# A hybrid attention and mLSTM network on one core: T4's low part by an adding DMA, keys' copies on GpSimd, and another order of the mLSTM heads' steps

## The chip, the cores and the metric

One core of a Trainium2 chip runs the whole program. TensorE (PE) multiplies; VectorE (DVE), ScalarE (ACT) and GpSimd (POOL) work on tiles; SyncE (SP) issues transfers, and so does GpSimd. Each engine works through its own instructions in their order and waits on the others by semaphores. The metric is the device time of one execution in microseconds (us). Of the kernel before, three runs are known.

## What is computed

```
h = x
h = h + dilated_attention_mixer(rms_norm(h, attn_norm[0]), positions, attn_w_in[0], attn_w_out[0])
h = h + swiglu(rms_norm(h, ffn_norm[0]), ffn_w_in[0], ffn_w_out[0])
h = h + mlstm_mixer(rms_norm(h, mlstm_norm[0]), mlstm_w_in[0], mlstm_conv_w[0], mlstm_conv_b[0],
                    mlstm_ig_bias[0], mlstm_fg_bias[0], mlstm_head_gain[0], mlstm_w_out[0])
h = h + swiglu(rms_norm(h, ffn_norm[1]), ffn_w_in[1], ffn_w_out[1])
return rms_norm(h, final_norm)

def swiglu(xn, w_in, w_out):
    gu = xn @ w_in
    return (jax.nn.silu(gu[..., :D_FF]) * gu[..., D_FF:]) @ w_out
```

512 tokens, a width of 1024. The attention has 8 heads of 128 in three groups of dilation 1, 4 and 16, with rotary turns of the first 32 of each head's dimensions. The mLSTM mixer has 8 heads too: queries and keys (64 wide) come out of a causal convolution with silu, each head's weights are exp of a difference of gate sums, times the scores, and its output is the weighted values over a denominator, normalized per head.

## The kernel before

Each fp32 operand is kept as a high and a low part, both of a rounded fp32 type; a product takes three matmuls (high by high, high by low, low by high). The high part is a copy that rounds (ACT); the low part is the difference to the raw value, as a rule one DVE operation.

**Feed-forward input.** From the column blocks j4 on, weights and tokens are multiplied with seven half-size products in place of eight (P1 to P7, `products`): sums and differences of weight blocks (A11 ... S4) times those of token blocks (B11 ... T4). The weight operands are made for each pair of blocks by `prepare` (load on SP, sum on DVE, high part on ACT, low part on DVE), the token operands once in each layer by `normalized`, whose steps are called between the products. `split_tokens` makes an operand's two parts. For B11 and T1 it uses the second way that it has (L1518 to L1520): ACT writes minus the high part, and an accumulating DMA issued by GpSimd adds the raw value. T4 is the last token operand and is read by the last product, P4. Its raw value T4 lies in the tile f0x (f1x in the second layer), whose buffer the weights of a later pair take (tag w8). In the trace the products of weights j4 are f0j_c, f0j_p and f0j_u; P2 adds into f0j_c, P7 and P4 into f0j_u, and between products ACT copies f0j_u out (f0j4u, L1680).

**Attention.** For each pair of heads the queries and keys of each group are projected, turned in `rope` and copied back into the operand tiles by the function `back` that `rope` returns. Group 0's copies go to GpSimd (L638), those of groups 1 and 2 to ACT (L642): 32 partitions by 512 elements for each of two queries' and two keys' halves (a1g_q, a1g_k in pair 1). Quarters 0 and 1 are the queries, 2 and 3 the keys. The copies are followed by the scores a1s (L781).

**mLSTM.** For each head hh `decay` makes the exponentials of gate differences (a matmul mHHnb into one bank, a mask on DVE, mHHd, ten exponentials on ACT, mHHe), `scores` makes queries times keys (mHHs, eight matmuls into two banks in turn) and multiplies them into mHHe on DVE (L2229), and `numerators` makes the weighted values (mHHnum, two banks of two), then a denominator, ACT's squares mHHj, a short row of DVE operations and the scaled output mHHyt (L2261). These steps are put off by `at_tick` to ticks that advance with the projections. Entries due at one tick run in the order in which they were queued. HEAD_AT gives the three ticks of each head:

```
HEAD_AT = ((9, 10, 12), (10, 11, 13), (12, 13, 15), (13, 14, 16), (15, 16, 18), (16, 17, 19), (18, 19, 21),
           (19, 20, 21))
```

A scheduler then sets the final order on each engine from the order in which the program issues and from its own estimate of times.

Of the kernel before, what the change touches and what calls it, by code (L numbers as in the profile page):

```python
# [40 lines left out]
HEAD_AT = ((9, 10, 12), (10, 11, 13), (12, 13, 15), (13, 14, 16), (15, 16, 18), (16, 17, 19), (18, 19, 21),  # L41
           (19, 20, 21))
# [32 lines left out]
def tile_hybrid_dilated_attn_mlstm(  # L75
# [4 lines left out]
    nc = tc.nc  # L80
# [336 lines left out]
    with ExitStack() as actx:  # L417
# [5 lines left out]
        R = 32  # L423
# [180 lines left out]
        def halves(t, th):  # L604
            return t[:, :, th * HALF:(th + 1) * HALF]
# [11 lines left out]
        def rope(qk, rot, blocks, first=0, end=4, direct=False):  # L617

            at = slice(R * first, R * end)
            a, sh = rot[0][at], rot[1][at]  # L620
            nc.vector.stream_shuffle(sh, a, shift)
            nc.vector.tensor_tensor(a, a, cosn[at], op=ALU.mult)
            nc.vector.tensor_tensor(sh, sh, sinn[at], op=ALU.mult)
            two_m = lambda t: t.rearrange("p (m s) -> p m s", m=2)
            if direct:
                for q in range(first, end):
                    nc.vector.tensor_tensor(halves(qk[q // 2][:R], q % 2), two_m(rot[0][quarter(q)]),
                                            two_m(rot[1][quarter(q)]), op=ALU.add)
                return
            nc.vector.tensor_tensor(a, a, sh, op=ALU.add)  # L630

            def back(by_pool=False):
                for q in range(first, end):
                    if blocks:
                        for m in range(2):
                            to, src = turned(qk, q, m, True), packed(rot, q, m, True)
                            if by_pool:
                                nc.gpsimd.tensor_copy(to, src)  # L638
                            else:
                                nc.scalar.activation(to, src, AF.Copy)  # L640
                    else:
                        nc.scalar.activation(halves(qk[q // 2][:R], q % 2), two_m(rot[0][quarter(q)]), AF.Copy)  # L642
            return back
# [325 lines left out]
        def qk_unit(pr, g, qk, then=None):  # L969
# [5 lines left out]
            rot = vu = None  # L975
# [51 lines left out]
            for n, name in enumerate(QK_ORDER):  # L1027
                key = target[name]
                if name in ("P1", "P5"):
                    acc[key] = acc_tile(nm + key)  # L1030
                if name == "P5":
                    acc["u"] = acc_tile(nm + "u")
                    nc.scalar.activation(acc["u"], acc["c11"], AF.Copy)
                    if g:
                        ahead_of_casts[0] = last_on(ACT)
                    feed.fill(feed.ahead + 1)
                whl = feed.pop()
                with fenced():
                    for m in range(2):
                        for k in range(4):  # L1040
                            for a, b in SPLITS:
                                if name in ("P1", "P2", "P4"):
                                    x_ = pair[b][k + 4 * (name != "P1")][:, HALF * (name == "P4"):HALF * (1 + (name == "P4"))]
                                else:
                                    x_ = sum_part(name, b, k)
                                nc.tensor.matmul(acc[key][:, m * HALF:(m + 1) * HALF], whl[a][:, k, m * P:(m + 1) * P], x_,
                                                 start=(name in ("P1", "P5") and m == 0 and k == 0 and (a, b) == SPLITS[0]),
                                                 stop=(m == 1 and k == 3 and (a, b) == SPLITS[-1]), skip_group_check=True)
                finish(name)
                if pr == 0:  # L1050
                    if g == 1:
                        if n == 0:
                            renew(range(4, 8))
                        elif n < 3:
                            sum_of("S%d" % (n + 2))
                        elif n == 6:
                            back = rope(qk, rot, False)
                            defer(1, lambda: behind(back, engine=ACT))
                            for key, hf in (("W11", 1), ("W12", 0), ("W12", 1), ("W22", 0), ("W22", 1)):
                                behind(load_block, 0, key, hf, engine=mybir.EngineType.SP)  # L1060
                    elif n == 6:
                        postponed.append(lambda: rope(qk, rot, False)())
                    if n in (1, 5):
                        advance()
                    continue
                if g == 2 and n == 2:
                    feed.ahead = 2
                if n == 6:
                    with behind_scores() if g == 2 else nullcontext():
                        back = rope(qk, rot, g == 0)  # L1070
                    if g == 0:
                        defer(1, lambda: back(True))
                    elif g == 2:
                        ahead_of_splits[0] = last_on(DVE)
                        back()
                        ahead_of_casts[0] = last_on(ACT)
                    else:
                        defer(1, lambda: behind(back, engine=ACT))
                if g == 2 and n == 5:
                    late[0] = last or by_products(pr + 1, 0)  # L1080
                    feed.fill(feed.ahead + 1)
                    late[0] = False
                if n in (1, 3, 5, 6):
                    advance()
                if n == 6 and then is not None:
                    then()
                if n:
                    feed.fill(feed.ahead + 1)
# [396 lines left out]
    def ffn_in(layer, fp, pair, rbc, hook, following, hid, during):  # L1485
# [27 lines left out]
        def split_tokens(key, by_dma=False):  # L1513

            i = [b for _, b in PRODUCTS].index(key)
            hi, lo = ops[key] = [op_tile(2 * i + part, key + "hl"[part]) for part in range(2)]
            nc.scalar.activation(hi, raw[key], AF.Copy)
            if by_dma:  # L1518
                nc.scalar.activation(lo, hi.bitcast(F32), AF.Copy, scale=-1.0)
                nc.gpsimd.dma_start(lo, raw[key], accum_op=ALU.add)  # L1520
            else:
                nc.vector.tensor_tensor(lo, raw[key], hi.bitcast(F32), op=ALU.subtract)

        def normalized():
            xs = [fp.tile([P, 4, SEQ], F32, tag="w8", name="f%dx%d" % (layer, i), bufs=2) for i in range(2)]
            for i in range(2):
                for t in range(2):
                    raw["B%d%d" % (i + 1, t + 1)] = xs[i][:, :, t * HALF:(t + 1) * HALF]
            for k in range(KC):
                nc.vector.scalar_tensor_tensor(xs[k // 4][:, k % 4], h[k], col("ffn", layer * KC + k), rbc,  # L1530
                                               op0=ALU.mult, op1=ALU.mult)
                yield
            split_tokens("B11", True)
            raw["T1"] = fp.tile([P, 4, HALF], F32, tag="t1", name="f%dt1" % layer)
            nc.vector.tensor_tensor(raw["T1"], raw["B12"], raw["B11"], op=ALU.subtract)
            yield

            split_tokens("T1", True)
            raw["T3"] = raw["B12"]
            nc.vector.tensor_tensor(raw["T3"], raw["B22"], raw["B12"], op=ALU.subtract)  # L1540
            yield
            split_tokens("T3")
            yield
            split_tokens("B22")
            yield
            raw["T2"] = raw["B22"]
            nc.vector.tensor_tensor(raw["T2"], raw["B22"], raw["T1"], op=ALU.subtract)
            split_tokens("T2")
            yield

            split_tokens("B21")
            yield

            raw["T4"] = raw["B21"]
            nc.vector.tensor_tensor(raw["T4"], raw["B21"], raw["T2"], op=ALU.subtract)
            split_tokens("T4")

        steps = normalized()
        STEPS = 2
# [461 lines left out]
    with ExitStack() as mctx:  # L2021
# [261 lines left out]
        def at_tick(t, fn):  # L2283
            defer(base + t - tick[0], fn)
        at_tick(8, exponents)
        for p, t in enumerate(STACK_AT):
            at_tick(t, lambda p=p: stack(p))
        for n, fn in enumerate((decay, scores, numerators)):
            for hh, ts in enumerate(HEAD_AT):
                at_tick(ts[n], lambda hh=hh, fn=fn: fn(hh))  # L2290
        for hh, t in LAST_OUTPUTS.items():
            at_tick(t, lambda hh=hh: outputs(hh))
        for pr, cs in ((2, (0, 2)), (3, (1, 3))):
# [254 lines left out]
```

## Time and profile before

| | us |
|---|---|
| median of 3 runs | 1383.32 (1382.18 to 1385.1) |
| the profiled execution | 1381.85 |
| its span | 1380.1 |
| attention with its output projection (awo) | 0 to 480 |
| first feed-forward (f0j on) | 480 to 846 |
| mLSTM mixer (mqk on) | 846 to 1038 |
| second feed-forward (f1j on) and the final norm | 1038 to 1380 |

The view of waits for TensorE lists each tile for which it stood still and what ended that wait; timelines show single instructions with their start; the view of windows shows each engine's busy time in a stretch. Line numbers are those of the kernel before; behind L634 the change adds two.

### The profile page before, as it was taken

The page shows a single profiled execution, that of the slowest core. Times are in us where ns is not written, and L with a number is a line of the kernel's source. Part 1 is how long each engine was busy: PE and PEld are TensorE (multiplying, and loading weights), DVE is VectorE, ACT ScalarE, POOL GpSimd, SP SyncE. Part 2 cuts the span into 40 slices and gives each one's busy share as a digit, 9 for nine tenths or more (in the row PEclk, how much of TensorE's full clock was granted, in tenths as well). Part 3 has the DMA queues.
Part 4 walks back from the last instruction along what each step waited for, and adds up shares of the span by engine and source line. Part 5 has one row for each costly group of instructions (what it writes and reads, how often), then busy time and mean ns, then how long its engine had stood idle before and what let it go on. Part 6 is the DMA issues. An engine that isn't in the chain of part 4 may idle for free. (4 is left out here: it accounts for less than half of the span.)

```text
span 1380.1 us, 23153 instructions
## 1 busy us (share of the span) xinstructions
PE 1363.8 (99%) x9028; PEld 1253.3 (91%) x9028; DVE 1127.4 (82%) x1782; ACT 806.2 (58%) x1297; POOL 183.0 (13%) x264
## 2 busy tenths in 40 slices
PE   9999999999999999999999999999999999999998
PEld 7898889999998889999999998888888899999886
DVE  7988668897975598788778799899858988887887
ACT  6766566777673444444476364786534544458854
POOL 3000013030402010000010110123102230001213
PEclk9999999999999999999999999999999999999999
DMA  9354245365576356323361743324334553335963
GB/s 311 112 176 137 92 139 184 130 183 169 172 264 208 105 139 167 123 73 111 123 167 63 168 125 92 92 64 121 92 123 122 148 174 115 123 113 131 200 162 106
DMA packets 140214, 193.85 MB, mean 140 GB/s; under 512 B 8996, under 2 KB 105060, under 8 KB 140104
## 3 DMA queue, kind: packets, MB, share of 16 engines
q1 hardware_dynamic: 120128, 140.73, 32.3%
q0 software_dynamic: 18752, 51.43, 15.4%
q8 instruction: 71, 1.16, 0.4%
q10 hardware_dynamic: 1224, 0.21, 0.1%
q14 instruction: 39, 0.32, 0.1%
HBM read 167.30 MB, written 22.54 MB: 138 GB/s over the span
## 5 line engine op out<-in xcount | busy, mean ns | idle before, releaser
L1805 POOL DMA_DIRECT2D f1T<-in_ffn_w_out_dram x15 | 17.8, 1185 | 207.7 <-DMA f1P_2w_w<-in_ffn_w_out_dram 136.4
L1780 POOL DMA_DIRECT2D f0S<-in_ffn_w_out_dram x10 | 8.7, 874 | 259.3 <-DVE f0hid L1697 173.2
L2337 POOL DMA_DIRECT2D hD<-hB x32 | 21.7, 697 | 68.5 <-DVE hB L2334 68.5
L268 PE MATMUL mo<-n_h,mo_k_l 128*128 128x512 f32 x64 | 25.3, 395 | 0.0
L268 PE MATMUL mo<-n_l,mo_k_h 128*128 128x512 f32 x64 | 25.2, 393 | 0.0
L268 PE MATMUL awo<-ao_h,awo_k_h 128*128 128x512 f32 x64 | 25.2, 393 | 0.0
L268 PE MATMUL mqk<-n_h,mqk_k_h 128*128 128x512 f32 x64 | 25.2, 393 | 0.0
L268 PE MATMUL mwo<-yo_l,mwo_k_h 128*128 128x512 f32 x64 | 25.1, 393 | 0.0
L268 PE MATMUL mo<-n_h,mo_k_h 128*128 128x512 f32 x64 | 25.1, 392 | 0.0
L268 PE MATMUL awo<-ao_h,awo_k_l 128*128 128x512 f32 x64 | 25.1, 391 | 0.0
L268 PE MATMUL f1j<-n_h,f1j_h 128*128 128x512 f32 x64 | 25.0, 391 | 0.0
L268 PE MATMUL f0j<-n_h,f0j_h 128*128 128x512 f32 x64 | 25.0, 391 | 0.0
L268 PE MATMUL mqk<-n_l,mqk_k_h 128*128 128x512 f32 x64 | 25.0, 391 | 0.0
L268 PE MATMUL awo<-ao_l,awo_k_h 128*128 128x512 f32 x64 | 25.0, 391 | 0.0
L268 PE MATMUL mqk<-n_h,mqk_k_l 128*128 128x512 f32 x64 | 25.0, 391 | 0.0
L268 PE MATMUL mwo<-yo_h,mwo_k_l 128*128 128x512 f32 x64 | 25.0, 391 | 0.0
L268 PE MATMUL f0j<-n_h,f0j_l 128*128 128x512 f32 x64 | 24.9, 390 | 0.0
L268 PE MATMUL f1j<-n_h,f1j_l 128*128 128x512 f32 x64 | 24.9, 390 | 0.0
L268 PE MATMUL f0j<-n_l,f0j_h 128*128 128x512 f32 x64 | 24.9, 389 | 0.0
L268 PE MATMUL f1j<-n_l,f1j_h 128*128 128x512 f32 x64 | 24.9, 389 | 0.0
L268 PE MATMUL mwo<-yo_h,mwo_k_h 128*128 128x512 f32 x64 | 24.9, 391 | 0.0
L233 DVE TENSOR_TENSOR v1P_l<-v1W,v1P_h 128x1024 fp32r<-128x1024 f32 x14 | 17.1, 1224 | 9.2 <-ACT v1P_h L231 9.1
(2716 smaller groups left out, 6006.6 us busy)
## 6 DMA issues: line engine op xcount, KB each, us to landing
f0j_w<-in_ffn_w_in_dram SPq DMA_DIRECT2D x17, 512.0 KB, 4.1
f1j_w<-in_ffn_w_in_dram SPq DMA_DIRECT2D x17, 512.0 KB, 6.0
f1T<-in_ffn_w_out_dram POOLq DMA_DIRECT2D x15, 512.0 KB, 7.0
f0hid<-in_ffn_w_in_dram SPq DMA_DIRECT2D x9, 512.0 KB, 5.6
f1hid<-in_ffn_w_in_dram SPq DMA_DIRECT2D x9, 512.0 KB, 5.3
v0W<-in_attn_w_in_dram SPq DMA_DIRECT2D x8, 512.0 KB, 6.8
v1W<-in_attn_w_in_dram SPq DMA_DIRECT2D x8, 512.0 KB, 3.7
awo_k_w<-in_attn_w_out_dram SPq DMA_DIRECT2D x8, 512.0 KB, 4.7
```

What stands on the lines that cost most here:

```text
L233: nc.vector.tensor_tensor(lo[:, :n], raw[:, :n], hi[:, :n].bitcast(F32), op=ALU.subtract)
L268: nc.tensor.matmul(acc, whl[a][:, k, m * P:(m + 1) * P], pairs[b][kk], start=(kk == 0 and (a, b) == SPLITS[0]), stop=(kk == nk - 1 and (a, ...
L1780: nc.gpsimd.dma_start(t, src[1][:, ks], accum_op=ALU.add)
L1805: nc.gpsimd.dma_start(view(to), weight_rows(hk * UNITS + u, n), accum_op=ALU.add)
L2337: nc.gpsimd.dma_start(hD[k // 4].rearrange("(b i) x -> i b x", i=R)[:, :, c0:c0 + R], t[R * a_:R * (a_ + 1)])
```

## The change

The diff:

```diff
             def back(by_pool=False):
                 for q in range(first, end):
-                    if blocks:
+                    if by_pool and not blocks and q > 1:
+                        nc.gpsimd.tensor_copy(halves(qk[q // 2][:R], q % 2), two_m(rot[0][quarter(q)]))
+                    elif blocks:
...
                     elif g == 2:
                         ahead_of_splits[0] = last_on(DVE)
-                        back()
+                        back(True)
                         ahead_of_casts[0] = last_on(ACT)
...
             nc.vector.tensor_tensor(raw["T4"], raw["B21"], raw["T2"], op=ALU.subtract)
-            split_tokens("T4")
+            split_tokens("T4", True)
...
         at_tick(8, exponents)
         for p, t in enumerate(STACK_AT):
             at_tick(t, lambda p=p: stack(p))
-        for n, fn in enumerate((decay, scores, numerators)):
-            for hh, ts in enumerate(HEAD_AT):
-                at_tick(ts[n], lambda hh=hh, fn=fn: fn(hh))
+        for hh in (4, 0, 1, 2, 3, 5, 6, 7):
+            for t, fn in zip(HEAD_AT[hh], (decay, scores, numerators)):
+                at_tick(t, lambda hh=hh, fn=fn: fn(hh))
```

T4's low part is made as B11's is, in both layers. The keys' copies of group 2 go to GpSimd in pairs 1 to 3, the queries' stay on ACT. The mLSTM heads' steps are queued head by head; where ticks tie, an earlier head's scores and numerators now come ahead of a later head's decay, but for head 4, whose decay stays ahead of head 2's numerators at tick 15.

How rows move. VectorE in the first feed-forward, around the split of T4, before (f0T4l is T4's low part, f0j4S_l and f0j4A_l those of weight operands):

```order
L233 TENSOR_TENSOR f0j4A_l<-f0j4A_5266,f0j4A_h 128x1024
L1522 TENSOR_TENSOR f0T4l<-f0x_5061,f0T4h 128x1024
L1629 TENSOR_TENSOR f0j4A_5266<-f0j4A_5266,f0j4S 128x1024
L233 TENSOR_TENSOR f0j4S_l<-f0j_w_5263,f0j4S_h 128x1024
L1629 TENSOR_TENSOR f0j6S<-f0j_w_5263,f0j6A_5445 128x1024
L233 TENSOR_TENSOR f0j4S_l<-f0j4A_5266,f0j4S_h 128x1024
L1629 TENSOR_TENSOR f0j_w_5263<-f0hid_5444,f0j_w_5263 128x1024
```

And with the change:

```order
L233 TENSOR_TENSOR f0j4A_l<-f0j4A_5266,f0j4A_h 128x1024
L1631 TENSOR_TENSOR f0j4A_5266<-f0j4A_5266,f0j4S 128x1024
L1631 TENSOR_TENSOR f0j6S<-f0j_w_5263,f0j6A_5446 128x1024
L233 TENSOR_TENSOR f0j4S_l<-f0j_w_5263,f0j4S_h 128x1024
L1631 TENSOR_TENSOR f0j_w_5263<-f0hid_5445,f0j_w_5263 128x1024
L233 TENSOR_TENSOR f0j4S_l<-f0j4A_5266,f0j4S_h 128x1024
```

f0T4l is gone; the difference f0j4A and then f0j6S follow at once on f0j4A_l, and the low part f0j4S_l of f0j_w comes behind f0j6S.

SyncE at the weight loads of the next pair in the same layer, with what each waits for, before:

```order
L1620 DMA f0j6A_5446<-in_ffn_w_in_dram 128x4x256 [waits DMAHW2_49,DVE_49]
L1620 DMA f0hid_5670<-in_ffn_w_in_dram 128x4x256 [waits DMAHW3_49]
L1620 DMA f0j_w_5669<-in_ffn_w_in_dram 128x4x256 [waits DMAHW4_49]
L1620 DMA f0j8A_5671<-in_ffn_w_in_dram 128x4x256 [waits DMAHW5_49,DVE_49]
L1620 DMA f0j8A_5672<-in_ffn_w_in_dram 128x4x256 [waits DMAHW6_49,DMAHW2_49,DVE_49]
```

And with the change, with a DMA of GpSimd's (DMASW5) as a new wait:

```order
L1622 DMA f0j6A_5447<-in_ffn_w_in_dram 128x4x256 [waits DMAHW2_49,DVE_49]
L1622 DMA f0hid_5671<-in_ffn_w_in_dram 128x4x256 [waits DMAHW3_49]
L1622 DMA f0j_w_5670<-in_ffn_w_in_dram 128x4x256 [waits DMAHW4_49,DMASW5_49]
L1622 DMA f0j8A_5672<-in_ffn_w_in_dram 128x4x256 [waits DMAHW5_49,DVE_49]
L1622 DMA f0j8A_5673<-in_ffn_w_in_dram 128x4x256 [waits DMAHW6_49,DMAHW2_49,DVE_49]
```

The third load takes the buffer of the tile f0x and now waits for the adding DMA that reads it, with two loads behind it.

TensorE in the mLSTM mixer, at head 0's scores and head 1's decay, before:

```order
L322 MATMUL mv_1_9130<-mv_k_h,n_l_8644 128x256
L2227 MATMUL m0s<-qs_0_9186,ks_0_9185 128x512
L2207 MATMUL m1nb<-mneg,sel 128x512
L2228 MATMUL m0s<-ql_0_9191,ks_0_9185 128x512
L2227 MATMUL m0s<-qs_0_9186,ks_0_9185 128x384
L2228 MATMUL m0s<-ql_0_9191,ks_0_9185 128x384
L268 MATMUL mqk_0_9313<-n_h_8637,mqk_k_h 128x512
```

And with the change:

```order
L322 MATMUL mv_1_9131<-mv_k_h,n_l_8645 128x256
L2229 MATMUL m0s<-qs_0_9187,ks_0_9186 128x512
L2230 MATMUL m0s<-ql_0_9192,ks_0_9186 128x512
L2229 MATMUL m0s<-qs_0_9187,ks_0_9186 128x384
L2230 MATMUL m0s<-ql_0_9192,ks_0_9186 128x384
L2209 MATMUL m1nb<-mneg,sel 128x512
L268 MATMUL mqk_0_9314<-n_h_8638,mqk_k_h 128x512
```

m1nb stands behind three more matmuls of m0s.

TensorE at head 1's numerators (mv are values' projections, mqk those of queries and keys), before:

```order
L322 MATMUL mv_0_9681<-mv_k_h,n_l_8640 128x256
L322 MATMUL mv_0_9681<-mv_k_h,n_h_8637 128x256
L322 MATMUL mv_0_9681<-mv_k_l,n_h_8637 128x256
L322 MATMUL mv_0_9681<-mv_k_h,n_l_8638 128x256
L2239 MATMUL m1num<-vaug,m1e 128x129 x10
L322 MATMUL mv_0_9681<-mv_k_h,n_h_8637 128x256
```

And with the change:

```order
L268 MATMUL mqk_0_9499<-n_h_8644,mqk_k_l 128x512
L268 MATMUL mqk_0_9499<-n_h_8644,mqk_k_h 128x512
L268 MATMUL mqk_0_9499<-n_l_8645,mqk_k_h 128x512
L268 MATMUL mqk_0_9499<-n_h_8644,mqk_k_l 128x512
L2241 MATMUL m1num<-vaug,m1e 128x129 x10
L268 MATMUL mqk_1_9500<-n_h_8642,mqk_k_h 128x512
L268 MATMUL mqk_1_9500<-n_l_8643,mqk_k_h 128x512
```

m1num stood among the values' matmuls behind m3s; it now stands 31 rows earlier, between two projections of queries and keys and ahead of m3s. Later in the mixer the same happens in smaller steps: nine instead of twelve matmuls of the output gate stand ahead of m4s's second use of a bank, and m3num moves 14 rows up.

## The prediction

> **What bounds the kernel now.** I read the page's busy shares first, then the view of waits for TensorE (engine, what it waited for, total us, times, longest), then timelines around those waits that the change touches.
>
> ```profile
> span 1380.1 us, 23153 instructions
> PE 1363.8 (99%) x9028; PEld 1253.3 (91%) x9028; DVE 1127.4 (82%) x1782; ACT 806.2 (58%) x1297; POOL 183.0 (13%) x264
> PE m1num L2239 <- DVE m0yt L2261: 1.2, 1, 1.2
> PE m1nb L2207 <- ACT m0e L2217: 1.0, 1, 1.0
> PE f0j_u L1658 <- ACT f0j4u L1680: 0.9, 1, 0.9
> PE f1j_u L1658 <- ACT f1j4u L1680: 0.8, 1, 0.8
> PE a1s L781 <- ACT a1g_k L642: 0.8, 1, 0.8
> ```
>
> TensorE is busy 1363.8 of 1380.1 us, so an edit is worth only what it does to TensorE's stalls. The five waits above, 4.7 us together, are those that the three edits aim at; no matmul is added or taken away. A saving on DVE or ACT counts for nothing unless TensorE stands still for it, and an added wait costs in full. Three edits, then: A, the low part of T4 made by ACT and an adding DMA instead of DVE; B, the keys' copies on GpSimd; C, the order of the mLSTM heads' steps.
>
> **A, layer 0.** Timeline rows are start, duration, engine, line, work; the two rows with "KB" are DMA issues and end in the us to landing; the last three rows are one-microsecond windows (busy times of PE, PEld, DVE, ACT, POOL) and end in the granted clock, the DMA share and GB/s.
>
> ```profile
> 536.40 0.28 PE L1658 MATMUL f0j_c<-f0B21h,f0j4A_l 128*128 128x256 f32 x1
> 537.63 0.39 PE L1658 MATMUL f0j_u<-f0T3h,f0j4S_h 128*128 128x256 f32 x1 [0.95 <-ACT f0j4u L1680]
> 533.57 1.22 DVE L1522 TENSOR_TENSOR f0T4l<-f0x,f0T4h 128x1024 fp32r<-128x1024 f32 x1
> 534.70 1.22 DVE L1629 TENSOR_TENSOR f0j4A<-f0j4A,f0j4S 128x1024 f32<-128x1024 f32 x1
> 536.04 1.06 ACT L231 ACTIVATE f0j4S_h<-f0j4A 128x1024 fp32r<-128x1024 f32 x1 [1.60 <-DVE f0j4A L1629]
> 537.00 0.58 ACT L1680 ACTIVATE f0j4u<-f0j_u 128x512 f32<-128x512 f32 x1
> 543.60 0.28 PE L1658 MATMUL f0j_u<-f0T4l,f0j4A_h 128*128 128x256 f32 x1
> 533.95 0.86 POOL L1780 DMA_DIRECT2D f0S<-in_ffn_w_out_dram  x1 [0.28 <-DVE f0j4A_l L233]
> f0T1l<-f0t POOLq DMA_DIRECT2D x1, 512.0 KB, 8.3
> f1T1l<-f1t POOLq DMA_DIRECT2D x1, 512.0 KB, 5.3
> 1072.00:1073.00 1.00, 1.00 (x6) 0.81 (x5) 1.00 (x2) 0.60 (x2) 1.00 (x3) 1.00 0.02 4
> 538.00:539.00 1.00, 1.00 (x11) 1.00 (x10) 1.00 (x2) 1.00 (x2) 0.00 (x0) 1.00 0.79 145
> 541.00:542.00 1.00, 1.00 (x11) 1.00 (x10) 1.00 (x2) 0.75 (x1) 0.00 (x0) 1.00 1.01 321
> ```
>
> The product P7 (f0T3 times f0j4S into f0j_u) waits 0.95 us for ACT's copy f0j4u, which stands on ACT behind the split f0j4S_h, which waited 1.60 us for DVE's difference f0j4A, which stood behind f0T4l. Without f0T4l, f0j4A starts at 533.57 instead of 534.70, 1.13 us earlier. ACT gets the copy f0T4l (1.06 us, as its 128x1024 splits) before that, and has the room: 1.60 us idle ahead of 536.04. With one split that it must now run between, f0j4S_h moves to about 535.3 and f0j4u to about 536.35, 0.65 us earlier. The low part that P7's third matmul reads keeps its place on DVE, since f0j6S moves into the room. So P7 gains 0.65 us.
>
> The price is in the DMA. P4 reads f0T4l at 543.60, at 542.95 once P7 is earlier. The adding DMA moves 512 KB. It can be issued when ACT's copy is done (about 533.95) and stands on GpSimd's queue behind the f0S row, so at 533.95 + 0.86 = 534.8. Its nearest rows are the same operation in each layer: 8.3 us beside weight loads, 5.3 us with little beside it. Of those 5.3, no transfer runs until 1073 (issue 1071.47; share 0.02 in the window quoted), so some 3.8 us are transfer. From 534.8 these give landings at 540.1 and 543.1. But the f0S transfers keep the engines busy until about 538.8 (share 0.79 in 538 to 539), and the next weight loads fill them from 541 (1.01). If the DMA begins to move when f0S is through, 2.2 of its 3.8 us are done at 541, and the other 1.6 us, at half the rate beside the loads, take 3.2: 544.2. I take the middle of 543.1 and 544.2, 543.6: the same moment at which P4 ran before, so the 0.65 us are given back as a wait for the DMA. Ends: -0.65 (in time) and +0.6 (544.2).
>
> The Trainium skill, page "DMA: Bandwidth & Descriptors", section "Two DMAs through the same engine are not ordered", says that descriptors of one queue on one engine start in order; by it the later of the two landings, 544.2, would hold and layer 0 would lose 0.6 us instead of nothing. No row before shows two such DMAs of one tile's size behind one another.
>
> The tile that the DMA reads is f0x, whose buffer the weight load f0j_w of the next pair takes, so SP now waits for the landing there:
>
> ```profile
> 540.34 0.50 SPq L1620 DMA_DIRECT2D f0j_w<-in_ffn_w_in_dram  x1
> L1629 DVE TENSOR_TENSOR f0j8S<-f0j_w,f0j8A x1: 1224/1224/1224, 553.0 to 553.0; 128x1024 f32<-128x1024 f32 x1
> ```
>
> f0j_w goes from 540.34 to about 543.7, and f0j8A behind it on SP to about 545. DVE wants both at 553.0; with 6 us to land there are 2 us to spare, so I cost this at nothing. If the DMA landed after 546, that cover would be gone.
>
> **A, layer 1.**
>
> ```profile
> 1091.92 1.18 DVE L1522 TENSOR_TENSOR f1T4l<-f1x,f1T4h 128x1024 fp32r<-128x1024 f32 x1
> 1094.16 1.22 DVE L233 TENSOR_TENSOR f1j4S_l<-f1j_w,f1j4S_h 128x1024 fp32r<-128x1024 f32 x1
> 1095.95 0.38 PE L1658 MATMUL f1j_u<-f1T3h,f1j4S_h 128*128 128x256 f32 x1 [0.85 <-ACT f1j4u L1680]
> 1092.70 2.66 POOL L2337 DMA_DIRECT2D hD<-hB  x4
> 1101.92 0.28 PE L1658 MATMUL f1j_u<-f1T4l,f1j4A_h 128*128 128x256 f32 x1
> ```
>
> The copy f1j4u comes earlier by the same steps, but the order of DVE changes too: the transpose hB and the difference f1j6S now stand ahead of the low part f1j4S_l, which the third matmul of P7 reads. It ended at 1095.38 and would end at about 1096.05, while that matmul ran at 1096.29. So P7 gains some 0.2 us, 0.15 with the small slips between engines that the rows show. The DMA goes ahead of the hD row at 1092.7 and with 5.3 us lands at 1098.0, 3.9 us before 1101.92; the hD issues are pushed back by about 1 us and have no reader that TensorE waits for. A together: -0.15 us, from -0.8 to +0.6.
>
> **B.** In pair 1 the scores (a1s) wait for the keys' copies; in pairs 2 and 3 no such wait is listed, so what moves there I cost at nothing (the scores come later than the copies).
>
> ```profile
> 251.33 2.36 DVE L946 TENSOR_TENSOR a2g0W<-a2g0W,a2g0W 128x1024 f32<-128x1024 f32 x2
> 252.79 1.28 ACT L642 ACTIVATE a1g_k<-rot 32x512 f32<-32x512 f32 x2
> 253.48 2.94 PE L781 MATMUL a1s<-a1g_k,a1g_q 128*128 128x128 f32 x24 [0.83 <-ACT a1g_k L642]
> 211.78 2.35 POOL L638 COPY a1g_q<-rot 32x256 f32<-32x256 f32 x4 [28.31 <-DVE rot L630]
> 281.16 4.69 POOL L638 COPY a2g_q<-rot 32x256 f32<-32x256 f32 x4 [3.19 <-DVE a1oth L828]
> ```
>
> On ACT the two key copies come after the two of the queries and end at 253.43 and 254.07. On GpSimd they need not wait for the queries' and can start at 251.4, when the rotation is done. The trace has no GpSimd copy of 512 elements. Copies of 256 took 2.35 us for four (0.59 each) and, beside a run of DVE's two-input 128x1024 operations, 4.69 us for four (1.17 each). For twice the elements I estimate 0.6 us (the first price, if most of it is fixed) to 1.2 (twice it). Here DVE runs two such operations from 251.33 to 253.69, so the second row is the nearer. Free of them, at 0.6: copies done at 252.0 and 252.6, and TensorE, which runs 24 matmuls in 2.94 us (0.12 each), goes through without its wait: 0.8 us earlier. Held up by each of the two: copies at 253.1 (0.33 earlier than before) and 254.75 (0.7 later). The changed order asks for the second copy after 12 matmuls, 1.47 us: 253.1 + 1.47 = 254.6, a wait of 0.15, then 16 more, 1.96: 256.7 against 253.48 + 2.94 = 256.4, so 0.2 to 0.3 us later. At 1.2 us a copy it would be 1.0. Value taken, by the nearer row: +0.2, ends -0.8 and +1.0.
>
> The Trainium skill, page "SBUF — State Buffer", section "Who interferes with whom", speaks against this edit: a DVE instruction with two SBUF inputs contends with a GpSimd instruction that reads SBUF, and the one that comes second blocks fully. By it the value would be the +0.2, without it -0.8; the trace agrees where the four copies took 4.69 us.
>
> **C.**
>
> ```profile
> 882.60 0.39 PE L2228 MATMUL m0s<-ql,ks 128*128 128x512 f32 x1
> 883.18 0.39 PE L268 MATMUL mqk<-n_h,mqk_k_h 128*128 128x512 f32 x1
> 902.74 0.35 ACT L2254 ACTIVATE m0j<-m0num,m0rr 128x128 f32<-128x128 f32 x1
> 914.20 1.11 DVE L2261 TENSOR_SCALAR m0yt<-m0num,m0rr 128x128 f32<-128x128 f32 x4
> 914.94 1.24 PE L2239 MATMUL m1num<-vaug,m1e 128*128 128x129 f32 x9 [1.25 <-DVE m0yt L2261]
> 933.10 1.77 DVE L2229 SCALAR_TENSOR_TENSOR m4e<-m4s,m4e 128x512 f32<-128x512 f32 x3
> 933.84 0.39 PE L2227 MATMUL m4s<-qs,ks 128*128 128x256 f32 x1
> ```
>
> m1nb, which waits 1.0 us for a bank, now stands behind the three m0s matmuls that followed it: 882.60 to 883.18, 0.58 us of work done inside the wait. Gain 0.58.
>
> m1num waits for DVE's m0yt (914.20), which frees the bank of the head before. m0yt hangs on ACT's m0j at 902.74 and a chain of DVE's small operations. The order moves m0j ahead of most of m2e, so about 1.6 us up, and m1num 31 rows up on TensorE: 12 matmuls of 0.23, 15 of 0.12 and m3s's four, 5.4 us. It was reached at 913.5 and will be at about 907.5, with the 0.58. Either the chain keeps up, since DVE no longer has other heads' work between its steps, or it does not and the wait grows. From the DVE rows between (about 6 us of other operations stand inside the chain and their order follows) I take m0yt at 907.3 to 908.3, and a wait of 0.2 instead of 1.25: gain 1.05.
>
> Given back: m4s, second bank use (933.84), starts as soon as the first of DVE's three m4e operations ends (933.10 + a third of 1.77, 933.7). TensorE now comes there three matmuls of the output gate (0.23 each, 0.68) and the 1.6 us won earlier. If DVE stays where it is, all 1.6 are lost and 0.68 more: C +0.7. If it moves along, nothing is lost: C -1.6. DVE's own work before it is two weight splits and the heads' chains, which move along in part: I take half of the 1.6 as lost, C -0.8. Two further loads of ACT's function table, which the new order brings, lie in ACT's idle time (58% busy).
>
> **Sum.** -0.15 + 0.2 - 0.8 = -0.75 us. The profiled execution took 1381.85 us (span 1380.1 and 1.75 around it), 1.5 below the median of the three runs, 1383.32. It would take 1381.1, the median 1382.55, so 1382.5. About 0.2% (2.8 us) is what a measurement here can tell from no change, and the forecast lies inside it.
>
> **Rivals.**
> 1. The stalls go and nothing is given back: the five rows, 4.7 us, of which A in layer 1 yields only 0.15 and A in layer 0 0.65: 0.65 + 0.15 + 0.83 + 1.6 = 3.2 us, 1380.1; with all 4.7, 1378.6. For it: each wait has its cause moved ahead. Against: B beside DVE's pair, and m4s. Chance 0.3.
> 2. Slower: the adding DMA in layer 0. It decides from the point at which it lands after 543.6, every microsecond later is one of TensorE's. If it moves only from 538.8 and takes as long as f0T1l in all, 8.3 us, it lands at 547.1: +3.5, and past 546 the SP loads behind it have no cover either. B and layer 1 nearly cancel; with C at nothing 1383.3 + 3.5 = 1386.8, with C at -0.8 1386.0. For it: the share of 0.79 and then 1.01. Against: f0T1l's 8.3 already hold its start and a heavy share. Chance 0.2.
> 3. All is given back, as waits merely move to the next reader in the mLSTM and to the landing: 1383.3. It lies inside the forecast's band, so I count it with the forecast: 0.5 for both.
>
> **Numbers.** Faster by over 0.2% needs rival 1, nearly whole: 0.3. Slower by over 0.2% is rival 2: 0.2. Within: 0.5. Low end: 1383.3 - 4.7 = 1378.6. High end: the upper ends of the terms (+0.6, +1.0, +0.7) give 1385.6, and rival 2 with C's gain carries it to 1386.0.
>
> **What would show it.** The wait of P7 in layer 0 falls from 0.95 to about 0.3, and P4 shows a wait for a DMA f0T4l of about 0.65; a landing before 542.9 proves the price wrong. In layer 1 the wait moves from ACT's f1j4u to DVE's f1j4S_l. In pair 1 GpSimd's two copies stretch beside L946, and the wait of a1s names GpSimd. m1nb's wait falls to 0.4, m1num's to 0.2, and m4s gets one of about 1 us. If m1num waits longer than before, C is wrong in sign.

## The result, and the profile after

Over 20 runs each, the kernel before took 1382.25 us (median; 1381.49 to 1385.1) and the changed one 1380.52 us (1378.54 to 1382.57). The medians lie 1.73 us apart; the ratio is 0.9986 (1.9 us), with a 95% interval from 0.998 to 0.9993. So the kernel is faster, clear of no change, but by less than the 0.2% that the prediction counts as no change. The time lies inside the range, and the case forecast (within 0.2%) came. That says little: the range, 1378.6 to 1386.0, also holds the kernel before. The size was off: the sum had -0.75 us. The profiled execution after took 1379.59 us, 2.26 us less than the one before.

The page of the changed kernel, its span and busy times:

```profile
span 1377.8 us, 23175 instructions
PE 1363.6 (99%) x9028; PEld 1252.3 (91%) x9028; DVE 1123.8 (82%) x1780; ACT 807.9 (59%) x1295; POOL 192.6 (14%) x272
```

TensorE's busy time stayed (1363.8 before), so all that went is idle time of TensorE. GpSimd's 9.6 us more of busy time cost nothing by themselves.

TensorE's waits in the changed kernel (engine, line, what it waited for: us in all, times, longest), those that bear on the edits:

```profile
PE m4s L2229 <- DVE m4e L2231: 0.9, 1, 0.9
PE a1s L783 <- POOL a1g_k L635: 0.9, 1, 0.9
...
PE m1nb L2209 <- ACT m0e L2219: 0.4, 1, 0.4
...
PE f0j_u L1660 <- ACT f0j4u L1682: 0.3, 1, 0.3
...
PE m6num L2241 <- DVE m5yt L2263: 0.2, 1, 0.2
...
PE f1j_u L1660 <- ACT f1j4u L1682: 0.2, 1, 0.2
...
PE f1j_u L1660 <- DVE f1j4S_l L233: 0.2, 1, 0.2
```

Line numbers behind the first edit are two higher than before. Of the five waits that the edits aim at, m1num's (1.2 us) is gone, m1nb's fell from 1.0 to 0.4, layer 0's f0j_u from 0.9 to 0.3, layer 1's f1j_u from 0.8 to 0.2 and another 0.2 on DVE. The wait of a1s is as long as it was and names GpSimd now. One wait is new: m4s, 0.9 us.

Where the time came from is read from the moments at which TensorE starts a given matmul, in the two profiled executions (start times in the timelines of TensorE):

| TensorE starts | before, us | after, us | after minus before | gained or lost since the row above |
|---|---|---|---|---|
| a1s, the scores of groups 1 and 2, pair 1 | 251.60 | 251.10 | -0.50 | -0.50 (nothing edited lies before it) |
| a2g0u, behind those scores | 256.18 | 255.74 | -0.44 | +0.06 (edit B, pair 1) |
| f0j_c, layer 0's product P2 | 533.64 | 532.79 | -0.85 | -0.41 (B in pairs 2 and 3, and what unedited stretches move) |
| f0j_u, layer 0's product P7 | 537.63 | 536.17 | -1.46 | -0.61 (edit A) |
| mqk, the mixer's first projection | 846.26 | 845.19 | -1.07 | +0.39 (A: P4 and what follows) |
| m0num | 896.17 | 894.32 | -1.85 | -0.78 (edit C: m1nb) |
| m2num | 927.94 | 924.72 | -3.22 | -1.37 (C: m1num) |
| mwo, the mixer's last projection | 994.06 | 991.34 | -2.72 | +0.50 (C: m4s) |
| finp, in layer 1's output projection | 1279.59 | 1276.65 | -2.94 | -0.22 (A in layer 1) |
| end of the span | 1380.1 | 1377.8 | -2.3 | +0.6 (nothing edited lies there) |

Edit C brings 1.65 of the 2.94 us, and A 0.22 in layer 0. The first 0.50 us belong to no edit: both kernels issue the same instructions up to there. Nor do the 0.6 us that are lost again behind finp, which is why the span is only 2.3 us shorter. The unedited stretches of the experiments below move by as much.

**Layer 0 after.** Timeline of TensorE, start and duration in us; the brackets give the idle time and what ended it:

```profile
536.17 0.39 PE L1660 MATMUL f0j_u<-f0T3h,f0j4S_h 128*128 128x256 f32 x1 [0.34 <-ACT f0j4u L1682]
542.12 0.28 PE L1660 MATMUL f0j_u<-f0T4h,f0j4A_h 128*128 128x256 f32 x1
542.44 0.39 PE L1660 MATMUL f0j_u<-f0T4l,f0j4A_h 128*128 128x256 f32 x1
542.66 0.28 PE L1660 MATMUL f0j_u<-f0T4h,f0j4A_l 128*128 128x256 f32 x1
542.78 0.28 PE L1660 MATMUL f0j_u<-f0T4h,f0j4A_h 128*128 128x256 f32 x1
```

Timeline of GpSimd's queue:

```profile
533.08 0.86 POOL L1782 DMA_DIRECT2D f0S<-in_ffn_w_out_dram  x1 [0.52 <-DVE f0j4A_l L233]
533.62 1.65 POOL L1522 DMA_DIRECT2D f0T4l<-f0x  x1
```

DMA issues of both layers (KB each, median us from issue to landing):

```profile
f0T4l<-f0x POOLq DMA_DIRECT2D x1, 512.0 KB, 8.8
...
f1T4l<-f1x POOLq DMA_DIRECT2D x1, 512.0 KB, 6.5
```

P7 waits 0.34 us instead of 0.95. P4's matmuls follow one another at 0.12 us, but the first that reads f0T4l comes 0.32 after its neighbour: 533.62 + 8.8 = 542.42, and it starts at 542.44. So TensorE stands still for the landing, though for only 0.2 us, too little for the list of waits. In layer 1 the issue at 1089.96 and the 6.5 us give 1096.5, and the reader starts at 1098.99: that landing costs nothing.

**Pair 1 after.** Timelines of DVE, GpSimd and TensorE, and GpSimd's copies in pairs 2 and 3:

```profile
250.85 2.77 DVE L948 TENSOR_TENSOR a2g0W<-a2g0W,a2g0W 128x1024 f32<-128x1024 f32 x2
251.09 3.00 POOL L635 COPY a1g_k<-rot 32x512 f32<-32x512 f32 x2 [9.82 <-DVE rot L630]
252.59 3.39 PE L783 MATMUL a1s<-a1g_k,a1g_q 128*128 128x128 f32 x28 [0.88 <-POOL a1g_k L635]
324.94 3.02 POOL L635 COPY a2g_k<-rot 32x512 f32<-32x512 f32 x2 [5.61 <-DVE rot L630]
400.34 1.27 POOL L635 COPY a3g_k<-rot 32x512 f32<-32x512 f32 x2 [6.54 <-DVE rot L630]
```

The views of these tiles, with the shortest, median and longest in ns, first before and then after:

```profile
L946 DVE TENSOR_TENSOR a2g0W<-a2g0W,a2g0W x2: 1220/1220/1220, 251.3 to 252.5; 128x1024 f32<-128x1024 f32 x2
L948 DVE TENSOR_TENSOR a2g0W<-a2g0W,a2g0W x2: 1218/1424/1630, 250.9 to 252.0; 128x1024 f32<-128x1024 f32 x2
L635 POOL COPY a1g_k<-rot x2: 1440/1469/1498, 251.1 to 252.6; 32x512 f32<-32x512 f32 x2
L635 POOL COPY a3g_k<-rot x2: 606/608/609, 400.3 to 401.0; 32x512 f32<-32x512 f32 x2
```

A copy takes 1.44 to 1.50 us where DVE runs two subtractions with two inputs beside it (pairs 1 and 2) and 0.61 us in pair 3, where DVE runs short operations of 128x128. DVE's pair took 2.77 us, 2.36 before; the first of the two took 1.22 us as before, and only the second, which starts at 251.99, is longer, 1.63 us.

**The mixer after.** Timelines of TensorE and DVE:

```profile
906.66 2.39 PE L2241 MATMUL m1num<-vaug,m1e 128*128 128x129 f32 x20
927.37 2.36 DVE L233 TENSOR_TENSOR mo_k_l<-mo_k_w,mo_k_h 128x1024 fp32r<-128x1024 f32 x2
930.32 1.14 DVE L2231 SCALAR_TENSOR_TENSOR m4e<-m4s,m4e 128x512 f32<-128x512 f32 x2
931.05 0.39 PE L2229 MATMUL m4s<-qs,ks 128*128 128x256 f32 x1 [0.93 <-DVE m4e L2231]
```

m1num runs without an idle bracket. m4s reuses a bank that the first m4e product frees, and that product stands on DVE behind two low parts of the output gate's weights (mo_k_l, 2.36 us) and a few short operations of head 2.

### The profile page after: what moved, and what is told of

Same layout as the page of the kernel before. It is cut to its first block, busy times and chain, and to the rows that moved or that the text cites. A ratio compares the mean times of both kernels' runs of the same rounds, so it can differ in the third digit from the quotient of the medians.

```text
span 1377.8 us, 23175 instructions
## 1 busy us (share of the span) xinstructions
PE 1363.6 (99%) x9028; PEld 1252.3 (91%) x9028; DVE 1123.8 (82%) x1780; ACT 807.9 (59%) x1295; POOL 192.6 (14%) x272
```

## The experiments

All times below stand beside runs of the kernel before on the same chip, taken in turn: its median was 1382.18 us beside the first four kernels, 1382.36 beside the next four, 1382.3 beside three of the last four and 1382.26 beside the last. Each has 11 runs, the last with the copies on GpSimd 7. "Stage" is the change of TensorE's lead over the kernel before between two rows of the table above, in the one profiled execution of each.

### Each edit alone

**A alone.** The kernel before, with this:

```
-            split_tokens("T4")
+            split_tokens("T4", True)
```

> Only T4's low part by the adding DMA, in both layers. My theory: P7 in layer 0 waits 0.3 us instead of 0.95, P4 there waits 0.2 to 0.3 us for the DMA (it lands just when P4 wants it); P7 in layer 1 waits 0.4 in two pieces instead of 0.85; sum -0.4 us, ratio 0.9997. Rival (the landing gives all back): P4 waits 0.65 and the sum is -0.15 or less. Rival (all stalls gone): -1.4 us, ratio 0.9990.

Measured: 1381.73 us, ratio 0.9995 (0.9987 to 1.0004). TensorE's waits in this kernel:

```profile
PE f0j_u L1658 <- DMA f0T4l<-f0x: 0.5, 1, 0.5
...
PE f0j_u L1658 <- ACT f0j4u L1680: 0.4, 1, 0.4
...
PE f1j_u L1658 <- DVE f1j4S_l L233: 0.2, 1, 0.2
```

The trade in layer 0 is there with both sides: P7's wait falls to 0.4, and P4 waits 0.5 us for the DMA, whose landing takes 9.1 us here. In its profiled execution layer 0 gave +0.31 and layer 1 -0.64.

**B alone.** The kernel before, with the edits at L633 and L1074 (GpSimd's copy for q > 1, and back(True)).

> Only the keys' copies on GpSimd. My theory: the two copies of pair 1 take 3.0 us beside DVE's two-input subtractions against 1.27 in pair 3 where none runs; the scores of pair 1 end as late as before, within 0.1 us, and the whole is within 0.2 us of before, ratio 1.0000. Rival (GpSimd saves ACT's time for TensorE): a1s loses its 0.8 us wait, ratio 0.9994.

Measured: 1382.17 us, 1.0004 (0.9996 to 1.0013). The scores of pair 1 waited 1.0 us for GpSimd's a1g_k, and the stretch of the scores lost 0.21 us. A new wait of 0.6 us in pair 3 (a3s for DVE's a3own) hangs on a weight load that came about 1 us later in this execution: the split of those weights began at 395.14 on ACT, 394.19 before. It isn't tied to the edit: the kernel below with the copies on ACT has such a wait of 0.8 us.

**C alone.** The kernel before, with the new order of the heads' steps.

> Only the order of the mLSTM heads' steps. My theory: nearly all of the gain is here, -1.65 us between the first projection of the mixer and its output projection (m1nb wait 0.4, no wait at m1num, 0.9 at m4s), ratio 0.9988. Rival (the gain is spread, or is the first 60 us of the program, which were 0.5 us shorter in the one profile): -0.8 us or less, ratio 0.9994 or above.

Measured: 1380.85 us, 0.9992 (0.9983 to 1.0001). Mixer -1.38 us; m1nb 0.4, no wait of m1num, m4s 0.9: as in the whole change.

By their medians the three parts add up: -0.5, 0 and -1.3 us are -1.8, and the whole has -1.7. By the ratios they are -0.7, +0.6 and -1.1, which is -1.2 against -1.9. The interval of each is about 1.2 us to either side, so this is agreement and no more.

**C with the heads in their plain order.** This tells whether it matters that head 4 comes first:

```
-        for n, fn in enumerate((decay, scores, numerators)):
-            for hh, ts in enumerate(HEAD_AT):
-                at_tick(ts[n], lambda hh=hh, fn=fn: fn(hh))
+        for hh in (0, 1, 2, 3, 4, 5, 6, 7):
+            for t, fn in zip(HEAD_AT[hh], (decay, scores, numerators)):
+                at_tick(t, lambda hh=hh, fn=fn: fn(hh))
```

> The heads' steps queued head by head in plain order 0 to 7, without head 4 first, and nothing else. ACT then runs head 2's four squares inside m4e. My theory: m4s keeps its wait of about 0.9 and its last part waits up to 0.5 more, so it is 0 to 0.5 us slower than the order with head 4 first, -1.2 to -1.65 us against before. Rival (head 4's decay ahead is what carries the gain): less than half of it is left, -0.8 us or less.

Measured: 1381.45 us, 0.9996 (0.9987 to 1.0005). Mixer -1.20 us, m4s 1.0. That is 0.2 us from C alone, and seven executions with the order of the change have -1.29 to -1.65, so neither the profile nor the times (0.6 us apart, on intervals of 1.2) tell the two orders apart.

### The prices taken away one by one

**T4's DMA ahead of the f0S rows.** The change, with the later adding DMAs of f0S issued behind that of T4 on GpSimd's queue:

```
+    t4_dma = [None]
...
                 nc.gpsimd.dma_start(lo, raw[key], accum_op=ALU.add)
+                if key == "T4":
+                    t4_dma[0] = last_on(mybir.EngineType.Pool)
...
-                nc.gpsimd.dma_start(t, src[1][:, ks], accum_op=ALU.add)
+                with tc.issue_after(t4_dma[0]) if t4_dma[0] is not None and u else nullcontext():
+                    nc.gpsimd.dma_start(t, src[1][:, ks], accum_op=ALU.add)
```

> The whole change, with T4's adding DMA in layer 0 ahead of the f0S transfers on GpSimd's queue. My theory (the landing is late because the DMA stands behind those transfers): it lands 5.5 to 7 us after its issue instead of 8.8, at least 1.5 us before P4, P4 has no wait for it, layer 0 gains 0.6 us between P2 and the next product instead of 0.2; ratio 0.9984. Rival (the landing is late because of the weight loads, whatever stands ahead): the DMA still takes 8 us or more and P4 still waits 0.2 to 0.5.

Measured: 1380.46 us, 0.9985 (0.9977 to 0.9994). The timeline of GpSimd's queue in this kernel:

```profile
536.23 1.29 POOL L1523 DMA_DIRECT2D f0T4l<-f0x  x1 [19.94 <-ACT f0T4l L1522]
536.99 3.24 POOL L1786 DMA_DIRECT2D f0S<-in_ffn_w_out_dram  x3
```

Its DMA issue:

```profile
f0T4l<-f0x POOLq DMA_DIRECT2D x1, 512.0 KB, 6.5
```

The three f0S rows (256 KB each) stand behind it now, and the landing takes 6.5 us instead of 8.8. P4 no longer waits, and layer 0 gives -0.45 us. The first matmul that reads f0T4l is on time in this execution and in the four later ones with this order; in the four with f0S ahead (the change, A alone and, below, keys on DVE and layer 0 only) it is late by 0.20, 0.65, 0.52 and 0.12 us. So the place in the queue makes that wait. The profile gains 0.2 us over the change in layer 0; the time shows nothing of it (1380.46 against 1380.52).

**The keys' copies on DVE.** The change, with DVE in GpSimd's place, ahead of its two subtractions:

```
-                        nc.gpsimd.tensor_copy(halves(qk[q // 2][:R], q % 2), two_m(rot[0][quarter(q)]))
+                        nc.vector.tensor_copy(halves(qk[q // 2][:R], q % 2), two_m(rot[0][quarter(q)]))
...
-                        ahead_of_splits[0] = last_on(DVE)
                         back(True)
+                        ahead_of_splits[0] = last_on(DVE)
```

> The whole change, but the keys' copies of the third groups by VectorE, straight behind the rotation and ahead of its two-input subtractions. My theory (GpSimd's copies lose to those subtractions for the SBUF port): the copies take 0.3 to 0.7 us each, a1s's wait of 0.9 falls to 0.2 or less, the scores of pair 1 end 0.7 to 1.0 us earlier than in the change; ratio 0.9980. Rival (the subtractions are pushed back by the copies and TensorE waits for their weights instead): the 0.9 us come back before the next pair's first products, ratio 0.9986.

Measured: 1380.75 us, 0.9989 (0.998 to 0.9998). Timelines of DVE and TensorE:

```profile
251.24 0.86 DVE L635 COPY a1g_k<-rot 32x512 f32<-32x512 f32 x2
251.99 3.39 PE L783 MATMUL a1s<-a1g_k,a1g_q 128*128 128x128 f32 x28 [0.66 <-ACT a1g_q L644]
256.03 0.39 PE L1048 MATMUL a2g0u<-S,a2g0P_l 128*128 128x256 f32 x1 [0.42 <-DVE a2g0P_l L233]
```

The two copies take 0.86 us instead of 3.00, and the scores wait for the queries' copy on ACT instead. The subtractions and the split behind the copies are later by as much, and a2g0u, whose weights they make, waits 0.42 us. The gain comes back one step on; the time is that of the change.

**Both together** (the two diffs above).

> The whole change with both: T4's DMA ahead of f0S and the keys' copies by VectorE. My theory: the two gains add, -0.4 and -0.8 on top of the change's -1.9, ratio 0.9978. Rival (a later wait takes them): ratio 0.9984 or above.

Measured: 1380.32 us, 0.9983 (0.9974 to 0.9991); T4's landing 6.1 us, m4s still 1.0. Neither price nor both together show in the time.

**m4e ahead of the second low part.** The last kernel, with one more order on DVE: the third mo_k_l behind head 4's first m4e product (mo_lows and first_of_4 are lists that collect these instructions as they are issued).

```
...
+        tc.add_manual_dep(mo_lows[2], first_of_4[0].name, mybir.DependencyInfo(
+            mybir.DependencyClass.NoSync, mybir.DependencyReason.DATA), reason="order")
```

> As e7_both, and the third low part of the output gate's weights on VectorE held behind the first product m4e of head 4. My theory (m4s waits because that low part stands ahead of m4e): the wait of m4s falls from 0.9 to 0.2 or less, -0.7 on top of e7. Rival (the squares and small operations of head 2 hold m4e, or the output gate then waits for the low part): m4s still waits 0.6 or more, or a wait of mo for mo_k_l appears; nothing on top of e7.

Measured: 1379.23 us, 0.9978 (0.997 to 0.9987), with the mixer at -2.73 us, 1.2 more than in the kernel that it was made from (-1.53). Timelines of DVE and TensorE:

```profile
930.32 0.68 DVE L2238 SCALAR_TENSOR_TENSOR m4e<-m4s,m4e 128x512 f32<-128x512 f32 x1
930.92 1.22 DVE L235 TENSOR_TENSOR mo_k_l<-mo_k_w,mo_k_h 128x1024 fp32r<-128x1024 f32 x1
931.05 0.39 PE L2236 MATMUL m4s<-qs,ks 128*128 128x256 f32 x1
```

The product comes ahead of one low part, and m4s starts without a wait. The median fell by 1.1 us as the profile did by 1.2, though the intervals of the two kernels overlap. Three executions with this order (the next two kernels have it too) give -2.73 to -2.79 us in the mixer, clear of the -1.29 to -1.65 without it: the give-back in C is this wait, and it can be had.

### Who should copy the keys, and which layer gains

**Copies on ACT, and copies on GpSimd, with the two orders added.** The first is the last kernel with the keys' copies on ACT as before; the second has them on GpSimd as in the change.

> As e8, with the keys' copies back on ScalarE as before the change. My theory (who copies the keys is worth nothing: GpSimd loses at the port, VectorE delays the subtractions, and all three end the scores of pair 1 within 0.3 us): the time of e8 within 0.3 us, ratio 0.9978 to 0.9980. Rival (the copies on VectorE or GpSimd free ScalarE and that counts): 0.6 us slower than e8 or more.

> As e8, with the keys' copies on GpSimd as in the change. My theory: as e9, within 0.3 us of e8; the two copies of pair 1 take about 3.0 us again and those of pair 3 about 1.3. Rival: 0.6 us slower than e8 or more.

Measured: 1379.72 us, 0.998 (0.9971 to 0.9989) on ACT, and 1378.82 us, 0.9973 (0.9962 to 0.9983) on GpSimd, where a1s waited 1.7 us in the profiled execution. With DVE's 1379.23, three engines lie within 0.9 us, inside one another's intervals: edit B has no size that these runs can tell. The version with GpSimd has the lowest median of all kernels here, 3.5 us under its own runs of the kernel before and 1.7 under the change's 1380.52; its interval and that of the change (0.998 to 0.9993) overlap a little, and it has 7 runs.

**T4's DMA in one layer only.** The change, with `split_tokens("T4", layer == 1)` in the first and `split_tokens("T4", layer == 0)` in the second.

> The whole change, but with T4's low part by VectorE in the first layer and by the adding DMA only in the second. My theory (in the first layer the landing takes back what P7 gains, 0.2 us of gain at the best and 0.4 of loss at the worst): from P2 to the next product as before the change, and the same time as the change within 0.3 us, ratio 0.9985 to 0.9988. Rival (the first layer carries the edit): 0.5 us slower than the change, ratio 0.9990.

> The whole change, but with T4's low part by the adding DMA only in the first layer and by VectorE in the second: the counterpart of e11. My theory (the first layer gives back what it gains, and the spread of the runs made e11 look slow): between P2 and the next product of the first layer -0.4 to +0.4 us as in the kernels before, the second layer as before the change, ratio 0.9985 to 0.9995. Rival (the first layer carries the edit in a way that the one profile of each kernel does not show): ratio 0.9986 or below, clear of e11's 0.9999, and more than 0.6 us gained in the first layer's products.

Measured: 1381.91 us, 0.9999 (0.999 to 1.0008) without the DMA in layer 0, and 1379.8 us, 0.9984 (0.9975 to 0.9993) with it there alone. The first missed what was expected of it; the second has the time of the rival (the first layer carries the edit) and the stages of the theory (it doesn't). By the medians the change loses 1.4 us when layer 0's DMA is taken out and gains 0.7 when layer 1's is; the profiled executions say otherwise, and that is taken up below.

The stages of the profiled executions, in us against the kernel before, over all kernels that bear on the question:

| stretch of TensorE | after | A alone | C alone | T4 ahead | layer 1 only | layer 0 only | best |
|---|---|---|---|---|---|---|---|
| start to a1s, pair 1 (nothing edited) | -0.50 | -0.48 | -0.13 | +0.55 | +0.26 | +0.12 | -0.36 |
| the scores of pair 1 | +0.06 | -0.09 | +0.10 | +0.48 | +0.35 | +0.64 | +0.84 |
| to layer 0's P2 | -0.41 | +0.32 | -0.27 | +0.76 | -0.47 | +0.14 | +0.83 |
| layer 0, P2 to mqk | -0.22 | +0.31 | -0.13 | -0.45 | 0.00 | -0.03 | -0.24 |
| mixer, mqk to mwo | -1.65 | -0.28 | -1.38 | -1.60 | -1.29 | -1.62 | -2.79 |
| layer 1, mwo to finp | -0.22 | -0.64 | -0.28 | -0.35 | +0.01 | -0.50 | -0.58 |

Stretches that a kernel leaves unedited (the first row, A alone in the mixer, C alone everywhere else, layer 1 where the edit is not in it) move by -0.50 to +0.55 us between the executions of the table, and over all executions by -0.87 (the first row, with the keys on DVE) to +0.81 (the third row, with the copies on ACT and the two orders added). The mixer's -1.29 and more stand clear of this. Layer 0's stretch by itself is quieter: without the edit it moves by -0.13 to +0.22, with f0S ahead of T4's DMA it gives -0.22, +0.31, +0.38 and -0.03, and in all five executions with T4 ahead -0.24 to -0.45.

## Why the prediction was right, and where its sizes were off

**The bound** held: TensorE's busy time is the same to 0.2 us, and every gain that is an edit's is a stall that went.

**The term that was most mis-sized is C**, -0.8 us predicted and -1.65 measured (-1.38 alone). The mechanism came as described. Of the 0.85 us between them, 0.5 are gains that were sized too low. m1nb was costed at 0.58 and gave 0.78 up to m0num. m1num was to keep 0.2 us of its wait and kept none, and a wait of 0.15 at m2num went too: up to m2num 1.37 us, not 1.05. The other 0.3 are the step "half of the 1.6 as lost": 0.50 were lost. The wait of m4s, "about 1 us", was 0.93, behind the mo_k_l splits, as the prediction had DVE stand; the order that puts m4e ahead shows it to be the cause. Counted from the mixer's start, TensorE came to that matmul 2.65 us earlier and m4e began 1.7 us earlier: DVE moved along by more than half. The 0.93 of m4s and 0.2 of m6num came, while m5num (0.2) and 0.3 of m6yT, listed before, went, so 0.6 net by the list of waits. The prediction let the loss at m4s last to the end, and did not count the small waits behind it that take up part of it.

**A in layer 0** was costed at nothing: 0.65 won at P7, 0.65 lost at P4. P7 gave 0.61. At P4 the reader came 0.2 us late, and 0.39 us in all were lost up to the mixer, so 0.22 are left in this execution and nothing over the four with this queue. The landing was costed at 543.6; it came at 542.42, in an execution that ran 0.85 us ahead, so at 543.3 on the clock of before, not before 542.9. The time from issue to landing was costed right, at 8.8 us (543.6 less 534.8), though only as the middle of two ends; 8.5 to 9.1 were measured. What was off is the issue: GpSimd issued it 0.54 us after the start of the f0S row (533.62 and 533.08), not after the 0.86 us that this row lasts. With f0S behind it the landing takes 6.0 to 6.5 us, so the place in the queue costs 2 to 3 us. The Trainium skill, page "DMA: Bandwidth & Descriptors", section "Two DMAs through the same engine are not ordered", says that one queue's descriptors on an engine start in order; the longer landing behind f0S agrees with that direction. The 9.4 us of the later end (544.2 less 534.8) did not come.

**A in layer 1** was -0.15: -0.22 in the profile, and its wait moved to DVE's f1j4S_l as said. The stretch gives -0.28 with C alone and -0.50 with A in layer 0 only, which both leave layer 1 untouched, so the edit's own share is about nothing. SP did wait for the landing in layer 0: f0j_w's load on SP's queue went from 540.34 to 542.41 (543.3 on the clock of before), where 543.7 was expected, and nothing on TensorE waits for it.

**B** was +0.2 and gave +0.06 in the change, +0.21 alone, and 0.4 on average over the six executions with GpSimd's copies (+0.06 to +0.84), where four other kernels with ACT's copies have 0.2 (-0.09 to +0.42). So the term was right, as far as this scatter tells. Its mechanism, "held up by each of the two", came as well. It put the ends of the copies at 253.1 and 254.75; they ended at 252.53 and 254.09 in an execution 0.50 us ahead there, so at 253.0 and 254.6 on the clock of before. The second was just in time for the matmuls that read it, and the 0.15 us of waiting for it did not come. The rows show how they meet: the first copy starts inside DVE's first subtraction, which takes its 1.22 us, and ends 0.5 us behind it; the second subtraction takes 1.63 us instead of 1.22; the second copy starts inside that one and ends 0.5 us behind it. Free of such a pair a copy takes 0.61 us. The Trainium skill, page "SBUF — State Buffer", section "Who interferes with whom", says that a DVE instruction with two SBUF inputs contends with a GpSimd instruction that reads SBUF, and that the one that comes second blocks until the other is through; these rows fit it. Even where the copies are cheap, on DVE, nothing is won: the weights behind the scores then wait.

**The rivals.** "All stalls go" (1380.1) came near in time, at 1380.52, but by luck and not as it was described: a1s still waits 0.9, m4s 0.9, m1nb 0.4. "Slower by the DMA" did not come: the reader was late by 0.1 to 0.65 us, not 3.5. The absolute forecast also stood on a median of three runs, 1383.32, of which 20 runs make 1382.25: 1.1 of the 2.0 us between 1382.5 and 1380.52 are that, and the rest is the sum's.

**What stays open.** The kernel with A in layer 1 alone took 1381.91 us and the one with A in layer 0 alone 1379.8, 2.1 us apart (the intervals overlap only from 0.999 to 0.9993), while their profiled executions, like that of A alone, give layer 0 between -0.2 and +0.4 us. A profile is one execution, and the landing lies within half a microsecond of its reader; that executions without a profile land in time and keep P7's 0.6 us would fit, but explains only a third of the distance, and moving the DMA ahead in its queue changed no time. Nor need all of it lie in layer 0: the slower one of the two has the new order of the mixer and -1.29 us there in its profile, as C alone has -1.38, and still its time fell by 0.4 us where that of C alone fell by 1.3. No run shows the cause.

## What to carry to other kernels

Where one engine is 99% busy, price an edit by the stalls it takes off that engine, then look along the same queue for the next reader of the same resource: m4s gave back half a microsecond of what m1num won, and one order on DVE brought 1.1 us of time. Moving a copy to an idle engine is worth nothing while a busy neighbour makes it twice as long, and the wait only moves. Read an edit of half a microsecond from the profile's own stage and from many runs, and trust it only where both agree.

## What the hardware showed that was not expected

- T4's adding DMA of 512 KB in layer 0 took 8.5 to 9.1 us behind three adding DMAs of 256 KB on the same queue, and 6.0 to 6.5 us ahead of them, in the same stretch of the program.
- GpSimd's copy of 32x512 took 1.44 to 1.50 us beside DVE's two-input subtractions of 128x1024 and 0.61 us in pair 3 without them. Of the two subtractions the first kept its 1.22 us and the second took 1.63, as if the two engines took turns, instruction by instruction.
- Up to the scores of groups 1 and 2 in pair 1, ahead of every edit, profiled executions differ by up to 1.4 us (-0.87 to +0.55 against the kernel before), and the wait of pair 1's scores was 0.9 to 1.7 us with GpSimd's copies unchanged.
